# Normalise four feature tiles first, run the second expert pass by tokens, and finish three layer norms late

## The chip, the cores and the metric

One core of a Trainium2 chip runs the whole program in one launch. The metric is device time in microseconds for one execution. Engines are called as in the profile: PE (TensorE matmuls) with PEld (its weight loads), DVE (VectorE), ACT (ScalarE), POOL (GpSimd) and SP (SyncE, which issues the DMAs).

## The reference, cut to what matters

256 tokens of width 1024 (plus 256 context tokens) pass through two blocks. The parts that the change touches:

```python
# block 1
m_l = silu(c) @ w_ada + b_ada            # six vectors of 1024: shift, scale, gate, twice
u_l = (layer_norm(x) * (1 + sc1) + sh1) @ w_in      # and the same for the context, with c_ctx
...                                       # two gated recurrences, w_out, layer norm
y   = peer(...)                           # 16384 experts; gates X[expert, token]
#   = gelu(U t) * gate, then  y[token, :] = sum over experts of X[expert, token] * V[expert, :]
x   = layer_norm(ALPHA * x + g2 * y)
# block 2: 16 meta tokens are put ahead (272 tokens), then twice
h = ln1(ALPHA_2 * h + 0.5 * swiglu(h, ffn1))
h = ln2(ALPHA_2 * h + mix(h @ w_in) @ w_out)
h = ln3(ALPHA_2 * h + 0.5 * swiglu(h, ffn2))
# swiglu: (silu(h @ w_gate) * (h @ w_up)) @ w_down, inner width 2816
```

## The kernel before, in words

Activations lie transposed: features on the 128 partitions, in 8 tiles of 128, tokens along the free axis. Every large product is computed in three matmuls (`mm3`, lines 326 to 328): both operands are split into a rounded part (fp32r) and the rest, and hi·hi, hi·lo and lo·hi are added up in PSUM.

**Weights** come as one stream, the class `Stream`: 512 KB tiles are loaded by SP into a ring of four buffers (`raw`, line 269), ACT writes the rounded part (`wh`, L292) and DVE, for some tiles POOL, the rest (`wl`, L293), two tiles ahead of use, each into a ring of three. A few tiles at the start of each feed-forward network are split earlier into spare buffers (`eh`, `el`), so that its first four tiles are at hand. Tiles of `w_ada` (`wa2`) come through the same ring and are used by DVE alone (`ada2_step`, L589). Pools and semaphores are the framework's; a planner orders the instructions of each engine at build time by program order and by when it takes their inputs to be ready, except where `issue_after` or `keep_in_program_order` binds them. On the chip each engine then runs in that fixed order.

**Front.** SP loads the first 1 MB tile of `w_ada` (`wa[0]`, of eight), then `xlat` and `xctx` (1 MB each), then three more `wa`, two weight tiles, four `wa`, and more weights (lines 469 to 472). DVE and ACT form sums and squares, PE adds them over the partitions (L527, L532), and `ada1_gen` gives shift and scale of four feature tiles a time (L501, L505, L508, L512); generators 0 and 1 serve tiles 0 to 3, 2 and 3 tiles 4 to 7. Lines 560 to 562 subtract the mean and multiply by `rstd` for all 8 tiles, in pieces of four tiles (128x1024), the product for the context on POOL. `modulate` (L543 to L545) gives `xh` and `xl` tile by tile. PE's first product is `fm_gen` (tiles 0 to 3, 512 tokens wide), then `ada1(2)`, `ada1(3)`, `modulate(3)`.

**Second expert pass.** For each of 128 turns, `w` is a 128x1024 tile of V and `x` the 128x256 gates of its 128 experts (`xsplit`, two turns ahead). `vmm` (L1214 to L1216) takes 128 columns of `w` as the stationary operand and the 256 tokens as the moving one, for 8 feature tiles d: 24 matmuls of 256 columns a turn, into four PSUM banks (`yv[d]` is half a bank). In turns 8 to 39 each fourth turn has an `ada2_step`. The last three turns go feature tile by feature tile; each then goes through L1232 (gate and residual) and `Stats.add`.

**Layer norm.** `Stats.add` (L370 to L387) sums tiles and squares; at the eighth tile PE adds them over the partitions with four fp32 products (L377, L378, L379, L383). `Stats.end` makes `r` (L392 to L395, `rsqrt_to`) and normalises the tiles in turn (L393, L400, L406); `to_input` gives the split input of the next product (L423 or L425 on ACT, L426 on POOL, L427), and the instructions named in `W.behind` hold later weight splits back. PE starts the next product with tile 0:

```python
        def ln_out(tp, st, l, j, tag="lnt", bufs=4):
            for k in st.end(eps1[:, 1:2], [hA[:, k] for k in range(8)]):
                n, g, b = hA[:, k], v2(l, f"ln{j}_g", k), v2(l, f"ln{j}_b", k)
                to_input(tp, k, n, g, b, hi_[:, k], lo_[:, k], tag, bufs)
```

This happens twice before the `mixers` and three times before a feed-forward network in block 2 (after `w_out` of each layer, and between the layers). `ffn` computes gate and up of the first two inner tiles together (`p4`, four weight tiles, 96 matmuls), then one inner tile f at a time, and last eight tiles of the down product. PSUM has 8 banks: four in turn for products (`PM`), four for the rest (`PS`; all four hold the sums of the second expert pass).

Of the kernel before, what the change touches and what calls it, by code (L numbers as in the profile page):

```python
# [171 lines left out]
def build(tc, A, out):  # L172
# [3 lines left out]
    with ExitStack() as ctx:  # L176
# [8 lines left out]
        def PS():  # L185
            return psum.tile([128, 512], F32, tag="aux", name="aux")
# [60 lines left out]
        class Stream:  # L247
# [112 lines left out]
        class Stats:  # L360


            def __init__(self, pl, N):
                self.pl, self.N = pl, N
                self.acc = pl.tile([128, N], F32, name="acc")
                self.acc2 = pl.tile([128, N], F32, name="acc2")
                self.k = 0

            def add(self, s):
                N, last = self.N, self.k == 7  # L370
                if self.k == 0:
                    self.s0 = s
                    S.activation(out=self.acc2, in_=s, func=AF.Square)
                else:
                    if last:
                        self.mean, self.ex2 = PS()[:, 0:N], PS()[:, 0:N]
                        T.matmul(self.mean, onesD, self.acc, start=True, stop=False)  # L377
                        T.matmul(self.ex2, onesD, self.acc2, start=True, stop=False)  # L378
                        T.matmul(self.mean, onesD, s, start=False, stop=True)  # L379
                    q = self.pl.tile([128, N], F32, name="sqk", tag="sqk", bufs=2)  # L380
                    S.activation(out=q, in_=s, func=AF.Square)  # L381
                    if last:
                        T.matmul(self.ex2, onesD, q, start=False, stop=True)  # L383
                    else:
                        V.tensor_tensor(self.acc, self.s0 if self.k == 1 else self.acc, s, OP.add)
                        (G if self.k < 5 else V).tensor_tensor(self.acc2, self.acc2, q, OP.add)  # L386
                self.k += 1  # L387

# [50 lines left out]
        with ExitStack() as fctx:  # L439
# [74 lines left out]
            a0 = ada1_gen(0)  # L514
            next(a0)
            a1 = ada1_gen(1)
# [31 lines left out]
            next(a1)  # L548
            for _ in a0:
                pass  # L550
            next(a1)
# [7 lines left out]
            for e in range(2):  # L559
                for a in range(0, 8, 4):  # L560
                    for src, st, op in ((xs[e], mean, OP.subtract), (xn[e], rstd, OP.mult)):
                        (G if e and st is rstd else V).tensor_tensor(xn[e][:, a:a + 4], src[:, a:a + 4], bc(st[:, None, 256 * e:256 * e + 256], [128, 4, 256]), op)
            W.split_to(0)
            modulate(1)

            lbt = const.tile([128, 3, 8], F32, name="lbt")
            V.tensor_tensor(lbt[:, 0], vc("hlb"), vc("hlb"), OP.subtract)
            S.activation(out=lbt[:, 0], in_=lbt[:, 0], func=AF.Exp)
            V.reciprocal(out=lbt[:, 1], in_=lbt[:, 0])
            V.tensor_tensor(lbt[:, 0], lbt[:, 0], lbt[:, 1], OP.mult)  # L570
            V.tensor_tensor(lbt[:, 0], lbt[:, 0], lbt[:, 0], OP.subtract)
            V.tensor_scalar(lbt[:, 0], lbt[:, 0], 0.0, 1.0 - 1e-6, op0=OP.max, op1=OP.min)
            V.tensor_scalar(lbt[:, 1], lbt[:, 0], LB_FLOOR, None, op0=OP.max)
            V.tensor_scalar(lbt[:, 2], lbt[:, 0], -1.0, 1.0, op0=OP.mult, op1=OP.add)
# [81 lines left out]
            for d in range(2):  # L656
# [7 lines left out]
                if d == 0:  # L664

                    gens = [fm_gen(512, ev, 2 * g) for g in range(2)]
                    W.LS = 0
                    next(gens[0])
                    ada1(2)
                    ada1(3)  # L670
                    modulate(3)
                    W.LS = 1
                    next(gens[1])
                    W.LS = 2
# [325 lines left out]
        with ExitStack() as ectx:  # L1000
# [208 lines left out]
            yv = [yacc[d // 2][:, 256 * (d % 2):256 * (d % 2) + 256] for d in range(8)]  # L1209

            def vmm(i2, d, w, x):
                c = slice(128 * d, 128 * d + 128)
                st_, sp_ = i2 == 0 and d % 2 == 0, i2 == 127
                T.matmul(yv[d], w[0][:, c], x[0], start=st_, stop=False, skip_group_check=True)  # L1214
                T.matmul(yv[d], w[0][:, c], x[1], start=False, stop=False, skip_group_check=True)  # L1215
                T.matmul(yv[d], w[1][:, c], x[0], start=False, stop=sp_, skip_group_check=True)  # L1216
            for i2 in range(125):
                w = W.get("s")
                xsplit(i2 + 2)
                x = xs_t.pop(i2)  # L1220
                for d in range(8):
                    vmm(i2, d, w, x)
                if 8 <= i2 < 40 and i2 % 4 == 0:
                    ada2_step(crow2)
# [3 lines left out]
            st = Stats(vp, 256)  # L1228
            for d in (0, 2, 4, 6, 1, 3, 5, 7):
                for i in range(3):  # L1230
                    vmm(125 + i, d, w[i], xs_t[125 + i])
                V.scalar_tensor_tensor(x1[:, d], yv[d], mada[:, 40 + d:41 + d], x1[:, d], op0=OP.mult, op1=OP.add)  # L1232
                st.add(x1[:, d])
# [25 lines left out]
        def ln_out(tp, st, l, j, tag="lnt", bufs=4):  # L1259
            for k in st.end(eps1[:, 1:2], [hA[:, k] for k in range(8)]):  # L1260
                n, g, b = hA[:, k], v2(l, f"ln{j}_g", k), v2(l, f"ln{j}_b", k)
                to_input(tp, k, n, g, b, hi_[:, k], lo_[:, k], tag, bufs)
# [12 lines left out]
        def ffn(l, j, last, after_first):  # L1275
            c0 = 16 if last else 0
            N = 272 - c0
            with tc.tile_pool(name="ffn", bufs=1) as tp:
                ah = tp.tile([128, 22, N], F32R, name="ah")
                al = tp.tile([128, 22, N], F32R, name="al")  # L1280
                for f in range(22):
                    if f == 0:
                        p4 = [PM()[:, 0:N] for _ in range(4)]
                        mm_pair(p4, [W.get("s") for _ in range(4)], c0, late=l == 0 and j == 1)
                        after_first()
# [11 lines left out]
                st = Stats(tp, N)  # L1297
# [10 lines left out]
                if not last:  # L1308
                    ln_out(tp, st, l, j)
# [13 lines left out]
        def mixers(l):  # L1323
            with tc.tile_pool(name="mx", bufs=1) as tp:
# [12 lines left out]
                mix = tp.tile([128, 8, 272], F32, name="mix")  # L1337
# [42 lines left out]
                proj(small_to, conv(0), conv(1), conv(2))  # L1380
                residual(3 * l, hA, hA)
# [76 lines left out]
                def attention(name, m0, qk, scale, v):  # L1458
                    PT = [tp.tile([128, 4, 272 - t0], F32, name=f"{name}T{j}", tag=f"attT{j}") for j, (t0, n) in enumerate(TT)]
                    units = [(0, 0), (1, 0), (1, 2), (2, 0)]  # L1460
                    P, mx = {}, {}
                    for u in units:
# [25 lines left out]
                        P[u] = tp.tile([128, 512], F32, name="attP", tag="attP", bufs=5)  # L1488
# [99 lines left out]
                def z_gate(f):  # L1588
                    def ev(p):
                        zs = tp.tile([128, 272], F32, name="zs", tag="zs", bufs=2)  # L1590
# [41 lines left out]
                st = Stats(tp, 272)  # L1632
# [6 lines left out]
                ln_out(tp, st, l, 2, "xb", 3)  # L1639
# [21 lines left out]
```

## Time and profile before

| | us |
|---|---|
| median of three runs | 2304.39 (2302.50 to 2306.07) |
| the profiled execution | 2302.7, of which the span of the trace is 2300.9 |
| PE busy | 2189.4 (95%) |
| DVE / ACT / POOL busy | 1547.5 / 1148.5 / 534.2 |
| second expert pass, first to last matmul | 832.3 to 1201.4 |

In the rows below a line of the timeline is: start, duration, engine, line, operation, output<-inputs, size, count, and in brackets the idle time ahead of it and what ended that. A matmul's duration is its way through the array; how often one starts is read from the starts of its neighbours. A row of the stretches gives the stretch, its length, the busy time of PE, PEld, DVE, ACT and POOL (with the number of instructions), the clock granted to PE as a share of 2.4 GHz, the share of time that DMA was busy, and GB/s.

### The profile page before, as it was taken

Reading aid. Unit: us, or ns where it says so; the run is one execution under the profiler, and the core shown is the slowest. Engines: PE = TensorE matmul, PEld = TensorE weight load, DVE = VectorE, ACT = ScalarE, POOL = GpSimd, SP = SyncE. Lnnn points to the kernel's source line nnn. Section 1 sums busy time; section 2 is a strip of 40 time slices with the busy share of each in tenths; the row PEclk is TensorE's granted clock in tenths of the full one; section 3 lists DMA queues with packets and bytes.
Section 4 is the critical chain, followed back from the end, with each engine's and each line's share of the span. In section 5 each row is a group of like instructions: output and inputs, shape, how many; then the busy total and the mean of one; then the engine's idle time right before and its main releaser. Section 6 shows DMA issues by size and latency. Waiting matters only on the chain.

```text
span 2300.9 us, 42996 instructions
## 1 busy us (share of the span) xinstructions
PE 2189.4 (95%) x17168; PEld 2116.5 (92%) x17168; DVE 1547.5 (67%) x2722; ACT 1148.5 (50%) x1976; POOL 534.2 (23%) x483
## 2 busy tenths in 40 slices
PE   6898889899999999999999999999999999899998
PEld 4787779899999999999999999889999999889998
DVE  6897869967677766555566556775556555776554
ACT  4455555344444454444445445565445444675443
POOL 2334334558666600000011002110001000302000
PEclk8999999999999999999999999999999999999999
DMA  6642125454444457655564554344564556233554
GB/s 260 230 166 74 56 85 166 138 169 153 148 155 152 152 189 228 201 183 184 182 216 149 174 171 149 101 138 147 174 179 152 174 170 197 92 120 122 188 179 126
DMA packets 102009, 367.55 MB, mean 160 GB/s; under 512 B 11440, under 2 KB 13360, under 8 KB 100528
## 3 DMA queue, kind: packets, MB, share of 16 engines
q1 hardware_dynamic: 101808, 364.80, 49.0%
q8 instruction: 134, 2.20, 0.4%
q14 instruction: 67, 0.55, 0.1%
HBM read 363.71 MB, written 1.05 MB: 159 GB/s over the span
## 4 chain that ended last, share of the span: by engine, by line
PE 83%; DVE 9%; issue 3%; POOL 2%; DMA 1%; ACT 1%; SPq 0%; DVEq 0%; POOLq 0%; ACTq 0%
PE main L328 20%; PE main L327 20%; PE main L326 20%; PE aux L1214 5%; PE aux L1215 5%; PE aux L1216 5%; PE aux L1106 2%; DVE wl L293 1%; DMA raw<-wa 1%; POOL wl L293 1%; DVE raw L589 1%; PE aux L808 1%; DVE acc L386 0%; PE aux L1526 0%; PE aux L1438 0%
## 5 line engine op out<-in xcount | busy, mean ns | idle before, releaser
L292 ACT ACTIVATE wh<-raw 128x1024 fp32r<-128x1024 f32 (+1 forms) x630 | 660.0, 1048 | 905.6 <-PE main L327 354.4
L293 DVE TENSOR_TENSOR wl<-raw,wh 128x1024 fp32r<-128x1024 f32 (+1 forms) x574 | 705.7, 1230 | 456.1 <-ACT wh L292 454.8
L326 PE MATMUL main<-hh,wh 128*128 128x256 f32 (+1 forms) x2856 | 826.7, 290 | 20.2 <-DVE hh L423 14.4
L328 PE MATMUL main<-hh,wl 128*128 128x256 f32 (+1 forms) x2856 | 822.3, 288 | 20.9 <-DVE wl L293 17.1
L327 PE MATMUL main<-hl,wh 128*128 128x256 f32 (+1 forms) x2856 | 821.2, 288 | 1.6 <-DVE hl L332 0.6
L328 PEld LDWEIGHTS main<-hh,wl 128*128 128x128 f32 x2856 | 546.4, 191 | 25.2 <-DVE wl L293 19.6
L326 PEld LDWEIGHTS main<-hh,wh 128*128 128x128 f32 x2856 | 545.6, 191 | 25.3 <-DVE hh L423 16.5
L327 PEld LDWEIGHTS main<-hl,wh 128*128 128x128 f32 x2856 | 545.6, 191 | 3.9 <-DVE hl L427 1.6
L1215 PE MATMUL aux<-xsl,wh 128*128 128x256 f32 x1024 | 290.2, 283 | 0.0
L1216 PE MATMUL aux<-xsh,wl 128*128 128x256 f32 x1024 | 290.0, 283 | 0.0
L1214 PE MATMUL aux<-xsh,wh 128*128 128x256 f32 x1024 | 289.9, 284 | 0.0
L386 POOL TENSOR_TENSOR acc<-acc,sqk 128x272 f32<-128x272 f32 (+1 forms) x32 | 40.7, 1271 | 852.0 <-ACT sqk L381 851.8
L1100 POOL TENSOR_SCALAR oh<-cst,slotT 128x128 f32<-128x128 f32 x256 | 209.8, 835 | 91.6 <-PE aux L1106 83.0
L326 PE MATMUL main<-ah,wh 128*128 128x272 f32 (+1 forms) x704 | 201.9, 287 | 0.0
L327 PE MATMUL main<-al,wh 128*128 128x272 f32 (+1 forms) x704 | 201.8, 287 | 0.0
L328 PE MATMUL main<-ah,wl 128*128 128x272 f32 (+1 forms) x704 | 201.3, 286 | 0.0
L293 POOL TENSOR_TENSOR wl<-raw,wh 128x1024 fp32r<-128x1024 f32 x56 | 151.2, 2704 | 214.5 <-ACT wh L292 203.5
L1215 PEld LDWEIGHTS aux<-xsl,wh 128*128 128x128 f32 x1024 | 196.8, 192 | 0.0
L1216 PEld LDWEIGHTS aux<-xsh,wl 128*128 128x128 f32 x1024 | 196.8, 192 | 0.0
L1214 PEld LDWEIGHTS aux<-xsh,wh 128*128 128x128 f32 x1024 | 196.6, 192 | 0.1
L328 PEld LDWEIGHTS main<-ah,wl 128*128 128x128 f32 x704 | 132.7, 189 | 0.0
L326 PEld LDWEIGHTS main<-ah,wh 128*128 128x128 f32 x704 | 132.6, 188 | 0.0
(470 smaller groups left out, 3138.3 us busy)
## 6 DMA issues: line engine op xcount, KB each, us to landing
raw<-uT SPq DMA_DIRECT2D x128, 512.0 KB, 3.3
raw<-pv SPq DMA_DIRECT2D x128, 512.0 KB, 3.5
raw<-ffn_gate SPq DMA_DIRECT2D x88, 512.0 KB, 3.3
raw<-ffn_up SPq DMA_DIRECT2D x88, 512.0 KB, 3.3
raw<-win SPq DMA_DIRECT2D x72, 512.0 KB, 3.4
raw<-ffn_down SPq DMA_DIRECT2D x64, 512.0 KB, 3.6
raw<-wa SPq DMA_DIRECT2D x32, 512.0 KB, 4.3
raw<-wout SPq DMA_DIRECT2D x24, 512.0 KB, 3.3
```

Source lines behind the costliest of these rows:

```text
L292: S.activation(out=hi[:, :n], in_=t[:, :n], func=AF.Copy)
L293: (G if mode == "p" else V).tensor_tensor(lo[:, :n], t[:, :n], hi[:, :n].bitcast(F32), OP.subtract)
L326: T.matmul(o, lh, rh, start=start, stop=False)
L327: T.matmul(o, lh, rl, start=False, stop=False)
L328: T.matmul(o, ll, rh, start=False, stop=stop)
L386: (G if self.k < 5 else V).tensor_tensor(self.acc2, self.acc2, q, OP.add)
L589: V.scalar_tensor_tensor(w, w, 1.0, c, op0=OP.mult, op1=OP.mult, accum_out=mada[:, 16 + j:17 + j])
L1100: G.tensor_scalar(oh1[:, j], iota, slotT[0][:, t0 + j:t0 + j + 1], None, op0=OP.is_equal)
L1106: T.matmul(pg[:, 128 * j:128 * j + 128], oh1[:, j], oh2[:, j], start=True, stop=True)
L1214: T.matmul(yv[d], w[0][:, c], x[0], start=st_, stop=False, skip_group_check=True)
L1215: T.matmul(yv[d], w[0][:, c], x[1], start=False, stop=False, skip_group_check=True)
L1216: T.matmul(yv[d], w[1][:, c], x[0], start=False, stop=sp_, skip_group_check=True)
```

## The change

Front: `xlat` and `xctx` are loaded ahead of `wa[0]`, and `ada1_gen(0)` and `(1)` run behind the statistics in program order. `normalise(a)` does four feature tiles: tiles 0 to 3 ahead of the first product, all on DVE; tiles 4 to 7 behind the first half of the first group, with the context's product on POOL. The lower bounds `lbt` are computed behind that.

Second expert pass: the gates of 128 tokens are the stationary operand and 512 columns of V the moving one; a turn has 12 matmuls, and `yacc` holds tokens by features. At the end the sums are copied out, transposed back on PE (`features`) and go on as before; `Stats` takes tiles 4 to 7 straight to PE (`pe=4`).

Late normalisation (`behind_norm`): for the norms after both `w_out` and after the second feed-forward network of layer 0, the un-normalised tile times the norm's gain (`gh`, `gl`: `raw_input`) is multiplied by the first four weight tiles, with two more columns (minus gain, and bias). The result is put right afterwards by mean and `r` (`finish`). `Stats` does its four products behind the 12th matmul of the first weight tile. `mix` and the attention's `attP` move into the memory of `gh` and `gl`. From the diff (cut):

```diff
-            load_wa()
             nc.sync.dma_start(xlat, A["xT"])
             nc.sync.dma_start(xctx, A["ctxT"])
-            for _ in range(3):
+            for _ in range(4):
                 load_wa()
...
-            a0 = ada1_gen(0)
-            next(a0)
-            a1 = ada1_gen(1)
+            a0, a1 = ada1_gen(0), ada1_gen(1)
...
+            def normalise(a):
+                for e in range(2):
                     for src, st, op in ((xs[e], mean, OP.subtract), (xn[e], rstd, OP.mult)):
-                        (G if e and st is rstd else V).tensor_tensor(...)
+                        E = G if a and e and st is rstd else V
+                        E.tensor_tensor(xn[e][:, a:a + 4], src[:, a:a + 4], ..., op)
+            normalise(0)
             W.split_to(0)
             modulate(1)
...
                     next(gens[0])
+                    W.split_to(1)
+                    normalise(4)
                     ada1(2)
                     ada1(3)
                     modulate(3)
...
+            def vmm(i2, e, w, x, ts=(0, 1)):
+                f = slice(512 * e, 512 * e + 512)
+                for t in ts:
+                    c = slice(128 * t, 128 * t + 128)
+                    y = yacc[2 * e + t]
+                    T.matmul(y, x[0][:, c], w[0][:, f], start=(i2 == 0), stop=False)
+                    T.matmul(y, x[0][:, c], w[1][:, f], start=False, stop=False)
+                    T.matmul(y, x[1][:, c], w[0][:, f], start=False, stop=(i2 == 127))
...
+            def half(e, t):
+                for i in range(3):
+                    vmm(125 + i, e, w[i], xs_t[125 + i], (t,))
+                if t == 0:
+                    S.activation(out=yt[:, 2 * e], in_=yacc[2 * e], func=AF.Copy)
+                else:
+                    V.tensor_copy(yt[:, 2 * e + 1], yacc[2 * e + 1])
+            def features(e):
+                for d in range(4 * e, 4 * e + 4):
+                    p = PM()[:, 0:256]
+                    for t in range(2):
+                        T.transpose(p[:, 128 * t:128 * t + 128], yt[:, 2 * e + t, c], ident)
+                    V.scalar_tensor_tensor(x1[:, d], p, mada[:, 40 + d:41 + d], x1[:, d], ...)
+                    st.add(x1[:, d])
+            half(0, 0); half(0, 1); half(1, 0); features(0); half(1, 1); features(1)
...
+        def raw_input(l, j, d):
+            S.activation(out=gh[:, d, r], in_=h_, func=AF.Identity, scale=g)
+            V.scalar_tensor_tensor(gl[:, d, r], h_, g, gh[:, d, r], op0=OP.mult, op1=OP.subtract)
+        def behind_norm():
+            def product(i):
+                p = PM()[:, 0:274]
+                hi, lo = W.get("s")
+                for k in range(8):
+                    mm3(p, hi[:, c], lo[:, c], gh[:, k], gl[:, k], k == 0, k == 7)
+                    if (i, k) == (0, 3):
+                        st.reduce()
+            def finish(i):
+                S.activation(out=cb, in_=p[:, 272:274], func=AF.Copy)
+                V.scalar_tensor_tensor(u, ms, cb[:, 0:1], p[:, 0:272], op0=OP.mult, op1=OP.add)
+                V.tensor_tensor(u, u, st.acc2, OP.mult)
+                S.activation(out=u, in_=u, func=AF.Identity, bias=cb[:, 1:2])
+            product(0); product(1)
+            for k in st.end(eps1[:, 1:2], [hA[:, k] for k in range(8)]):
+                to_input(b2, k, ...)       # k == 1: ms = copy of the mean
+                ...                        # k == 2: finish(0); k == 4: finish(1)
+            product(2); product(3); finish(2); finish(3)
```

## Rows read from the trace of the kernel before

**Rows 1.** The page: busy time by engine, and the chain's shares.

```profile
PE 2189.4 (95%) x17168; PEld 2116.5 (92%) x17168; DVE 1547.5 (67%) x2722; ACT 1148.5 (50%) x1976; POOL 534.2 (23%) x483
...
PE 83%; DVE 9%; issue 3%; POOL 2%; DMA 1%; ACT 1%; SPq 0%; DVEq 0%; POOLq 0%; ACTq 0%
```

**Rows 2.** Stretches: length; PE, PEld, DVE, ACT, POOL busy (count); clock; DMA; GB/s.

```profile
37.17:350.00 312.83, 274.66 (x1830) 241.05 (x1831) 258.87 (x406) 164.97 (x267) 117.45 (x70) 0.94 0.35 117
...
832.30:1201.40 369.10, 369.10 (x3075) 368.80 (x3073) 213.02 (x285) 179.68 (x266) 5.53 (x7) 1.00 0.62 198
...
1545.97:1556.71 10.74, 7.13 (x34) 5.92 (x33) 8.69 (x22) 6.04 (x12) 4.04 (x6) 0.84 0.16 50
1556.71:1752.82 196.11, 196.11 (x1561) 196.11 (x1561) 106.14 (x134) 92.31 (x129) 8.50 (x9) 1.00 0.55 175
1752.82:1761.50 8.68, 5.64 (x26) 4.66 (x25) 6.56 (x17) 4.96 (x10) 4.49 (x5) 0.80 0.20 62
...
2093.83:2102.90 9.07, 5.79 (x25) 4.55 (x24) 7.10 (x18) 4.73 (x10) 3.38 (x5) 0.81 0.18 59
```

**Rows 3.** Timeline of PE in the second expert pass, first and last of 49.

```profile
1000.05 0.28 PE L1216 MATMUL aux<-xsh,wl 128*128 128x256 f32 x1
...
1005.81 0.28 PE L1216 MATMUL aux<-xsh,wl 128*128 128x256 f32 x1
```

**Rows 4.** Timeline of PE, matmuls of 512 columns, first and last of 13.

```profile
61.25 0.40 PE L327 MATMUL main<-xl,wh 128*128 128x512 f32 x1
...
63.98 0.39 PE L327 MATMUL main<-xl,wh 128*128 128x512 f32 x1
```

**Rows 5.** Waits, 840 to 1190 us: who waited for whom, us, times, longest.

```profile
ACT wh L292 <- PE aux L1215: 182.1, 121, 1.5
```

**Rows 6.** The page: DMA issues of V, KB each, us from issue to landing.

```profile
raw<-pv SPq DMA_DIRECT2D x128, 512.0 KB, 3.5
```

**Rows 7.** Timeline at the end of the second expert pass, all engines.

```profile
1201.16 0.28 PE L1216 MATMUL aux<-xsh,wl 128*128 128x256 f32 x1
...
1202.21 2.35 POOL L293 TENSOR_TENSOR wl<-raw,wh 128x1024 fp32r<-128x1024 f32 x1 [1.33 <-ACT wh L292]
...
1202.54 2.30 DVE L386 TENSOR_TENSOR acc<-acc,sqk 128x256 f32<-128x256 f32 x1
...
1205.70 1.06 PE L383 MATMUL aux<-sqk,onesD 128*128 128x256 f32 x2
...
1209.57 0.60 PE L326 MATMUL main<-hh,e 128*128 128x272 f32 x1 [2.80 <-DVE hh L423]
```

**Rows 8.** Groups by line and form, 1440 to 1545 us: PE transposes.

```profile
L1411 PE MATMUL aux<-cst,cv 128*128 128x128 f32 x8 | 1.0, 273 | 0.0
```

**Rows 9.** Timeline of the front, all engines.

```profile
7.15 1.93 PE L501 MATMUL aux<-x,cs 128*32 128x512 f32 x8 [3.76 <-DMA x<-wa]
...
9.55 1.23 DVE L524 TENSOR_TENSOR s<-xlat 128x1024 f32<-128x1024 f32 x1 [2.71 <-DMA xlat<-xT]
...
16.89 1.22 DVE L562 TENSOR_TENSOR xn<-xlat,aux 128x1024 f32<-128x1024 f32 x1 [0.40 <-ACT m2a L555]
...
21.36 1.11 PE L532 MATMUL aux<-sq,onesD 128*128 128x256 f32 x4
...
27.41 6.15 POOL L562 TENSOR_TENSOR xctx<-xctx,rstd 128x1024 f32<-128x1024 f32 x2 [26.97 <-ACT rstd L336]
27.98 6.66 DVE L562 TENSOR_TENSOR xn<-xn,rstd 128x1024 f32<-128x1024 f32 x2
...
34.57 0.70 DVE L544 TENSOR_SCALAR xm<-xn,mada 128x256 f32<-128x256 f32 x1
...
37.17 0.79 PE L327 MATMUL main<-xl,wh 128*128 128x512 f32 x1 [3.92 <-DVE xl L545]
```

**Rows 10.** Groups by line and form around the first late norm, 1545.5 to 1562 us.

```profile
L427 DVE TENSOR_TENSOR hl<-t,hh 128x272 fp32r<-128x272 f32 x8 | 3.7, 477 | 1.5 <-POOL t L426 1.1
...
L383 PE MATMUL aux<-sqk,onesD 128*128 128x272 f32 x2 | 0.6, 393 | 0.0
```

More of the change, by code (lines that the diff above doesn't have):

```diff
@@ L360, in build, with __init__ @@
         class Stats:
[L363 to L366, printed above, removed]
+            def __init__(self, pl, N, bufs=1, late=False, pe=7):
+                self.pl, self.N, self.late, self.pe = pl, N, late, pe
+                self.acc = pl.tile([128, N], F32, name="acc", tag="acc", bufs=bufs)
+                self.acc2 = pl.tile([128, N], F32, name="acc2", tag="acc2", bufs=bufs)
                 self.k = 0
@@ L673, in build @@
                     next(gens[1])
+                    lower_bounds()
                     W.LS = 2
@@ L1220, in build @@
                 x = xs_t.pop(i2)
-                for d in range(8):
-                    vmm(i2, d, w, x)
+                for e in range(2):
+                    vmm(i2, e, w, x)
                 if 8 <= i2 < 40 and i2 % 4 == 0:
@@ L1257, in build, with raw_columns @@
         V.memset(onesG, 1.0 / 256)
-        def ln_out(tp, st, l, j, tag="lnt", bufs=4):
+        pending, raw = [], [None, None]
+        def raw_columns(l, j):
+            gh, gl = raw[:] = [b2.tile([128, 8, 274], F32R, name=n, tag=n) for n in ("gh", "gl")]
+            for c, n, s_ in ((272, "g", -1.0), (273, "b", 1.0)):
+                v = v2(l, f"ln{j}_{n}", 0, 8)
+                S.activation(out=gh[:, :, c], in_=v, func=AF.Copy, scale=s_)
+                V.scalar_tensor_tensor(gl[:, :, c], v, s_, gh[:, :, c].bitcast(F32), op0=OP.mult, op1=OP.subtract)
@@ L1264, in mm_pair @@
+                if k == 4:
+                    finish(1)
+            product(2)
+            product(3)
+            finish(2)
+            finish(3)
+            return out_
         def mm_pair(outs, ws, c0, order=range(8), x=(hi_, lo_), late=False):
@@ L1282, in ffn @@
                     if f == 0:
-                        p4 = [PM()[:, 0:N] for _ in range(4)]
-                        mm_pair(p4, [W.get("s") for _ in range(4)], c0, late=l == 0 and j == 1)
+                        if pending:
+                            p4 = [u[:, c0:] for u in behind_norm()]
+                        else:
+                            p4 = [PM()[:, 0:N] for _ in range(4)]
+                            mm_pair(p4, [W.get("s") for _ in range(4)], c0, late=True)
                         after_first()
@@ L1296, in ffn @@
                 ln_exp_table()
-                st = Stats(tp, N)
+                late = not last and j == 3
+                st = Stats(b2, N, 1, late)
+                if late:
+                    raw_columns(l, j)
                 for d in range(8):
@@ L1307, in ffn @@
                     st.add(h_)
-                if not last:
-                    ln_out(tp, st, l, j)
+                    if late:
+                        raw_input(l, j, d)
+                if late:
+                    pending.append((st, l, j))
+                elif not last:
+                    for k in st.end(eps1[:, 1:2], [hA[:, k] for k in range(8)]):
+                        to_input(b2, k, hA[:, k], v2(l, f"ln{j}_g", k), v2(l, f"ln{j}_b", k), hi_[:, k], lo_[:, k], "lnt", 3)
                 else:
```

106 lines of the change are left out of this document (67 added, 39 removed).

## The prediction

> **What bounds the kernel now.** I read the page's shares of busy time and the chain first, then the stretches of the span, then the timeline where PE stands still. PE is busy 95% of the span and carries 83% of the chain [rows 1], so there are two ways to win time: fill the 111.5 us in which PE idles (2300.9 less 2189.4), or make its matmuls fewer. In the second expert pass PE never idles: 369.1 us busy of 369.1 at full clock [rows 2]. There only the matmuls' own pace counts. The other places this change touches are gaps: PE's first real matmul comes at 37.17 us [rows 9], and three layer norms in block 2 leave stretches of 10.74, 8.68 and 9.07 us in which PE is busy 7.13, 5.64 and 5.79 us, at a granted clock of 0.84, 0.80 and 0.81, that is, partly at the lower of its two levels, 1.2 GHz, after it stood still [rows 2].
>
> **Second expert pass: 19.5 us less for the matmuls.** Matmuls of 256 columns start each 5.76 us / 48 = 0.120 us [rows 3]. Matmuls of 512 columns with the same kinds of operand (fp32r, 128x128 stationary, another stationary tile each time) start each 2.73 / 12 = 0.2275 us at full clock [rows 4], not 0.240: some 12 ns a matmul don't grow with its columns. A turn goes from 24 x 0.120 = 2.88 to 12 x 0.2275 = 2.73 us; 1536 x 0.2275 = 349.4 us against 3072 x 0.120 = 368.6, which is 19.2 less. Against the measured 369.1 it is 19.7; rounding of the starts leaves both open by about 1 us either way, and I take 19.5.
>
> The Trainium skill (TensorE: Matmul & The Clock Gate, section Back-to-back issue gap) states that the gap between matmuls of N columns is N/2.4 ns plus about 2.5 ns at full clock. By it 3072 gaps of 109 ns become 1536 of 216 ns, an estimate of 3.8 us gained instead of 19.5. The trace disagrees with the page for this stream: 120 ns, not 109, at 256 columns [rows 3], and 227.5, not 216, at 512 [rows 4]; I go by the rows.
>
> Can the operands keep up with a turn of 2.73 us? DVE is busy 213.0 / 128 = 1.66 us a turn and ACT 1.40 [rows 2], and neither gets more of it. ACT's split waited for PE to free its buffer in 121 of the 128 turns [rows 5]. A tile of V lands 3.5 us after its issue [rows 6] and four buffers give it four turns, 10.9 us, for that and two splits. So supply stays hidden; in the eight turns with an `ada2_step` five tiles must come in 10.9 us, which is 2.2 us each, and there the reserve is least.
>
> **The end of that pass: 2.5 us more.** The sums now lie tokens by features. Behind the last matmul come a copy out of PSUM (128x512, at most twice a 272-wide DVE operation of 0.477 us [rows 10]: 0.95), and before it on DVE up to 1 us left over from `features(0)`, whose nine operations of about 0.45 us don't fit beside the six 512-column matmuls and transposes that cover them. Then transposes (16 x 0.125 us = 2.0 us on PE [rows 8], half of them ahead of the last group of matmuls), and four tiles that each need two fp32 products, at 0.5 us each (0.6 for one by itself [rows 10]): 4.0 us, where before the four products of the end were all that was left. Before, the last square's product starts at 1205.70, 4.5 us behind the last matmul at 1201.16 [rows 7]. Of this, about 1.9 us went into a DVE addition that took 2.30 us beside a POOL subtraction of 2.35 [rows 7]; with `pe=4` no such addition stands there. After: 1.0 + 0.95 + 0.5 (first transposes and gate) + 4.0 + 0.6 = 7.0 us, and 1 us of transposes ahead of the last group: 3.5 more, or, where DVE clears in time, 1.5. I take 2.5. The norm behind it is unchanged. Net for the pass: 17.
>
> **Front: 7 us less.** `xlat` landed at 9.55 us, one megabyte behind `wa[0]` at 7.15 [rows 9]; loaded first it lands some 2.4 us earlier and `xctx` too. `wa[0]` moves back two places in SP's queue, by 2 x 2.4 us, but `wa[1]` to `wa[3]`, on which generators 0 and 1 end, come behind the same bytes as before. So the statistics gain 2.4 us, and perhaps 1 us more, since their last matmuls (21.36 [rows 9]) no longer run among generator work. From `rstd`, ready at 27.41, to the first `xl` DVE and POOL do both halves of the context and the latent: 6.66 us for two DVE products that take 1.22 us each when POOL is quiet (the row at 16.89 is the same shape), because POOL's two (6.15 us) run beside them [rows 9]. Now DVE does two of 1.22 us for tiles 0 to 3 and goes on to `modulate`; PE then starts 2.6 us after the first `xm` (34.57 to 37.17), as before. That is 6.66 - 2.44 = 4.2 us less. One POOL product of about 3 us is left for tiles 4 to 7, and as the planner may put it first, DVE can lose up to 3 us to it; a weight subtraction (1.2 us) can also fall between. Together 2.4 + 1 + 4.2 = 7.6 at the most likely order, 2.4 if POOL and the shifts eat the rest, 11 if the weight split slips behind too. I take 7. Tiles 4 to 7 then fall where DVE had little to do, behind the first 24 matmuls; `lbt` is small work that only has to be there by the first gates. From 37 to 350 us DVE is busy 258.9 of 312.8 us and PE 274.7 [rows 2]: neither is full, the stages hang on one another, so an earlier start moves them all.
>
> The Trainium skill (SBUF — State Buffer, section SBUF: two separate sides) has the lock that this looks like: a DVE operation with two SBUF inputs and a GpSimd operation that reads SBUF don't share, the second blocks until the first ends. By it the one POOL product that stays can cost its whole length, about 3 us, and the front would give 4 rather than 7; the trace agrees with the lock at 1202.54, 2.30 us for a 256-wide addition [rows 7].
>
> **Three late norms: 9 us less.** What a gap costs now: its length, less its main matmuls at 196.11 / 1561 = 0.1256 us [rows 2], less the four statistic products that remain (2.0 us at 0.5). The first stretch holds 34 PE instructions, of which 8 are the statistics (each product is two) and 2 straddle its edges: 10.74 - 24 x 0.1256 - 2.0 = 5.7. The second: 8.68 - 16 x 0.1256 - 2.0 = 4.7. The third: 9.07 - 15 x 0.12 - 2.0 = 5.3. Sum 15.7: the ceiling, for PE that never waits. Added: two columns in 272 are nothing, but the last network has 256 columns and now gets 274 in four weight tiles: 96 x 0.0056 = 0.5 us. `raw_input` adds an ACT and a DVE operation (about 0.6 and 0.48 us) per tile; beside 24 matmuls, 3.0 us, DVE comes to about 3.0 us a tile behind `w_out`, so up to 0.5 us may be late; behind the down product (66 matmuls, 8.3 us) it is hidden. For the last tile the wait for `gl` is covered: 21 matmuls and the statistics (2.6 + 2.0 us) stand ahead of its use.
>
> What is late next: PE has 96 x 0.126 + 2.0 = 14.1 us of work behind the last tile, and its next matmuls need the eighth normalised tile 2.6 us later, at 16.7. DVE starts the norm at about 3.6 us, spends some 2.3 us to the first normalised tile, then 10 us on eight tiles (three operations of 0.45 us each, 10.8, of which one or two lie ahead) and 4 x 0.47 = 1.9 us on `finish(0)` and `(1)`, so the eighth is there at 17.8. Behind it the held-back weight subtraction (1.2 us) reaches 19.0, and the second product of that inner tile wants it at 18.3. So 1.1 + 0.7 = 1.8 us wait, each time, 5.4 in all; PSUM banks come free earlier, at `finish(0)`. 15.7 - 0.5 - 5.4 - 0.8 (DVE behind `w_out`) = 9. Bounds: 15 if the planner finds room, 2 if `finish` and the splits queue badly.
>
> **Sum.** 17 + 7 + 9 = 33 us off the profiled execution's 2302.7 us: 2269.7. The median of the runs is 1.7 above it, so 2271 us.
>
> **Rivals.**
> - *The pass gains nothing*, because what a matmul costs beyond its columns doubles with them (0.240 us each): 2302.7 + 2.5 - 16 + 1.7 = 2291. For it: no 512-column stream of V as the moving operand is in the trace. Against: in [rows 4] all kinds of operand are alike, at full clock. (The Trainium skill's gap rule above is a milder form of it, with an estimate of 2287.)
> - *The norms give nothing*: DVE is late by the whole 5 us each time, 2280. For it: DVE has 8.69 us of work in 10.74 already [rows 2] and gets more. Against: PE gets 12 us of work that needs none of it.
> - *The front is taken back later*: an earlier start meets loads that are not there; 2278. For it: neither PE nor DVE is full from 37 to 350 us, so one slow transfer there can take up a head start. Against: DMA is busy 0.35 of that stretch [rows 2], and its ring places are freed by work that starts earlier as well.
> - *Slower: the ring of four is late in every turn of the second pass.* Place: SP's issue of V's next tile, which waits for DVE's subtraction. Each 0.1 us by which a turn exceeds 2.73 costs 12.8 us; from 2.99 us a turn all 33 us are gone, and at 3.1 the time is 2271 + 47 = 2318. Against: the same ring fed turns of 2.88 us with ACT always waiting for PE [rows 5], at 198 GB/s [rows 2], and 2.73 needs 209.
> - *It doesn't do what it says*: pass and norms both give nothing and the front's 7 us pay for the pass's longer end: 2304.4 - 7 + 2.5 = 2300.
>
> **How the numbers follow.** The forecast 0.62 (own range 2261 to 2281); norms give nothing 0.12; front taken back 0.12; pass gains nothing 0.06; nothing in sum 0.04; slower 0.04. A difference under 0.2%, 4.6 us, can't be told from none in this kernel. Faster by more: 0.92; within: 0.04; slower: 0.04. The range takes in the bounds of front and norms and the first three rivals: 2256 to 2288.
>
> **What would show it.** Starts of 512-column matmuls in the pass 0.2275 us apart (0.24: the first rival), the pass 350 us long, ACT still waiting for PE; from its last matmul to the next product some 10 to 11 us instead of 8.4; PE's first `xl` matmul near 30 us; no idle PE and clock 1.0 behind each `w_out`, and a wait for `hl` of about 1 us some 14 us later. It is wrong if PE waits for `wl` in the pass, or if the time stays above 2288.

## The result, and the profile after

The changed kernel takes 2282.8 us (median of four executions, 2274.6 to 2283.0) against 2304.7: ratio 0.9891, 95% interval 0.988 to 0.9903: 21.9 us less by the medians, 25 by the ratio. The forecast was 2271 us, 33.4 less, with a range of 2256 to 2288. Two more measurements of the same kernel (below, again and again_2) gave 0.9879 [0.9862, 0.9897] and 0.9876 [0.986, 0.9893]; over the 12 executions its mean is 2280.0 us and they spread from 2274.6 to 2283.5. So the gain is about 27 us, some 6 less than forecast, and the first three unprofiled executions lay at the high end.

The profiled execution took 2274.6 us (span 2272.5). The page's shares after, to be read beside [rows 1]:

```profile
PE 2171.7 (96%) x15660; PEld 2037.1 (90%) x15660; DVE 1576.2 (69%) x2776; ACT 1167.2 (51%) x2035; POOL 527.8 (23%) x479
...
PE 80%; DVE 11%; issue 4%; ACT 2%; POOL 2%; DMA 1%; SPq 0%; POOLq 0%; DVEq 0%; ACTq 0%
```

The stretches that answer to [rows 2]: the second expert pass, then each late norm from the last matmul of the product before it to the point where PE no longer waits:

```profile
829.49:1178.97 349.48, 349.48 (x1547) 289.00 (x1546) 220.09 (x279) 180.26 (x264) 0.79 (x1) 1.00 0.64 205
1527.96:1548.30 20.34, 19.21 (x140) 18.15 (x139) 19.27 (x45) 16.87 (x36) 6.43 (x9) 1.00 0.17 56
1731.22:1751.50 20.28, 19.15 (x140) 18.09 (x139) 17.72 (x42) 16.69 (x36) 7.23 (x9) 1.00 0.17 56
2068.40:2088.70 20.30, 18.98 (x140) 17.96 (x139) 19.29 (x45) 16.83 (x36) 6.42 (x9) 1.00 0.18 58
```

PE is busy all through the pass, 349.5 us instead of 369.1, and ACT still waits for it, as in [rows 5]. In this trace the clock in the norms is 1.00 where it was 0.80 to 0.84 (the last section has others), and PE idles 1.1 to 1.3 us in 20 where it idled 3.0 to 3.6 in 9 to 11.

PE in the pass, first and last of 16 matmuls of 512 columns, and who waited from 840 to 1170 us (us, times, longest):

```profile
999.62 0.39 PE L1232 MATMUL aux<-wh,xsh 128*128 128x512 f32 x1
...
1003.02 0.39 PE L1232 MATMUL aux<-wh,xsh 128*128 128x512 f32 x1
```

```profile
ACT xsh L331 <- PE aux L1233: 163.9, 122, 1.4
```

(1003.02 - 999.62) / 15 = 0.2267 us from start to start.

Where the 28.4 us between the spans of the two profiled executions come from, read as the shift of the same instruction in both traces:

| stretch | us |
|---|---|
| up to the pass's first matmul (832.33, now 829.49) | -2.8 |
| the pass, first to last matmul (368.83, now 349.25) | -19.6 |
| its end, last matmul to next product (8.41, now 12.44) | +4.0 |
| the three late norms | -3.7, -2.7, -2.6 |
| all the rest behind the pass | -1.0 |

### The profile page after: what moved, and what is told of

It is laid out like the page before. It is cut to its first block, busy times and chain, and to the rows that moved or that the text cites. A ratio compares the mean times of both kernels' runs of the same rounds, so it can differ in the third digit from the quotient of the medians.

```text
span 2272.5 us, 40212 instructions
## 1 busy us (share of the span) xinstructions
PE 2171.7 (96%) x15660; PEld 2037.1 (90%) x15660; DVE 1576.2 (69%) x2776; ACT 1167.2 (51%) x2035; POOL 527.8 (23%) x479
## 4 chain that ended last, share of the span: by engine, by line
PE 80%; DVE 11%; issue 4%; ACT 2%; POOL 2%; DMA 1%; SPq 0%; POOLq 0%; DVEq 0%; ACTq 0%
PE main L328 19%; PE main L326 19%; PE main L327 19%; PE aux L1233 5%; PE aux L1232 5%; PE aux L1234 5%; PE aux L1122 3%; DVE wl L293 2%; DVE raw L602 1%; POOL wl L293 1%; PE aux L824 1%; ACT wh L292 0%; PE aux L1632 0%; PE aux L1543 0%; DMA raw<-win 0%
## 5 line engine op out<-in xcount | busy, mean ns | idle before, releaser
L328 PE MATMUL main<-hh,wl 128*128 128x256 f32 (+1 forms) x2808 | 807.9, 288 | 22.2 <-DVE wl L293 18.3
L326 PE MATMUL main<-hh,wh 128*128 128x256 f32 (+1 forms) x2808 | 812.5, 290 | 12.4 <-DVE hh L436 5.7
L327 PE MATMUL main<-hl,wh 128*128 128x256 f32 (+1 forms) x2808 | 805.8, 287 | 1.9 <-DVE hl L440 0.8
L327 PEld LDWEIGHTS main<-hl,wh 128*128 128x128 f32 x2808 | 534.8, 190 | 4.1 <-DVE hl L440 1.8
L388 POOL TENSOR_TENSOR acc<-acc,sqk 128x272 f32<-128x272 f32 (+1 forms) x29 | 37.3, 1287 | 1210.8 <-ACT sqk L381 1210.7
L1232 PE MATMUL aux<-wh,xsh 128*128 128x512 f32 x512 | 199.3, 390 | 0.0
L1233 PE MATMUL aux<-wl,xsh 128*128 128x512 f32 x512 | 199.3, 389 | 0.0
L1234 PE MATMUL aux<-wh,xsl 128*128 128x512 f32 x512 | 199.2, 389 | 0.0
L331 ACT ACTIVATE xsh<-X 128x256 fp32r<-128x256 f32 x128 | 53.4, 418 | 166.1 <-PE aux L1233 164.3
L327 PEld LDWEIGHTS main<-al,wh 128*128 128x128 f32 x704 | 132.2, 188 | 0.0
L1119 DVE TENSOR_SCALAR oh<-cst,slotT,slotT 128x128 f32<-128x128 f32 x256 | 80.6, 357 | 55.3 <-PE aux L1122 55.3
```

Source lines behind the costliest of these rows:

```text
L326: T.matmul(o, lh, rh, start=start, stop=False)
L327: T.matmul(o, lh, rl, start=False, stop=False)
L328: T.matmul(o, ll, rh, start=False, stop=stop)
L331: S.activation(out=hi, in_=src, func=AF.Copy)
L1119: V.tensor_scalar(oh2[:, j], iota, slotT[1][:, t0 + j:t0 + j + 1], slotT[2][:, t0 + j:t0 + j + 1], op0=OP.is_equal, op1=OP.mult)
L1232: T.matmul(y, x[0][:, c], w[0][:, f], start=(i2 == 0), stop=False)
```

## The experiments

All kernels of one group ran on one chip beside the kernel before, whose executions there spread from 2302.4 to 2311.1 us. Ratios are to it, and "us less" is worked out from the ratio.

**The parts by themselves, and the whole once more.**

> The changed kernel once more, nothing edited. Its profiled execution took 2274.6 us, the other three 2282.7 to 2283.0. Theory A: an execution falls into one of two courses some 8 us apart; the repeat shows times near 2274.6 and near 2282.8 and nothing between, most of them the longer one, and if its profile falls into the longer course, one stage of the trace carries the whole 8 us as idle PE. Rival B: the first time was a stray; all times lie from 2281 to 2285. Rival C: the times are spread evenly from 2274 to 2284, many small delays.

Measured: 2278.9 us (2277.4 to 2282.5), 0.9879 [0.9862, 0.9897]. There are no two groups: with the first four and again_2, twelve executions in all fill 2274.6 to 2283.5 without a gap of 2 us. C holds.

Front alone: the diff's hunks ahead of the second expert pass.

> The kernel before with the front's part of the change alone (the loading order, four tiles normalised ahead of the others, the lower bounds later). Forecast on record: 7 us less. My theory now: in the trace of the changed kernel PE's first product with xl comes 5.1 us earlier, but behind 320 us only 2.8 us of it are left, so alone it gives 2.8 us: 2301.9 as a median. Rival: the loss is a matter of the two other parts (they do not touch the front, but the planner's times do), and alone it gives 5 us or more: 2299 or less. Second rival: the longer course of the changed kernel comes from the front; then this median is 5 us above the kernel before, near 2310, while its shortest time is 2.8 below.

Measured: 2303.0 against 2306.9, 0.9983 [0.9974, 0.9992]; 3.9 us less, 1.8 to 6.0 by the interval. That holds the theory's 2.8 and the first rival's 5, and not the 7 on record. The eleven executions, 2301.2 to 2305.8, show no longer course.

Pass alone: `vmm`, `half`, `features` and `Stats`.

> The kernel before with the second expert pass by tokens alone, and its statistics with four tiles taken to PE. Forecast on record: 17 us less (matmuls 19.5 less, the end 2.5 more). My theory now: 15.6 less (matmuls 19.6 less, the end 3.9 more, because POOL's weight subtraction blocks a DVE addition there): 2289.1. Rival: the pass at 209 GB/s is where the longer course of the changed kernel comes from, a tile of V that is late now and then; then the median is some 2297 and the trace or the times show two groups 8 us apart.

Measured: 2290.3 (2285.6 to 2296.0, without two groups), 0.9926 [0.991, 0.9943], 17 us less; the interval holds both the 17 on record and the 15.6. The matmuls take 349.24 us in this trace, the end 13.78.

Norms alone: `behind_norm`, `raw_input`, `raw_columns` and the buffers, and with them the order of the first products behind the norms that stay as they were.

> The kernel before with the three late norms alone (and the order of the first products behind the norms that stay as they were). Forecast on record: 9 us less. My theory now: 9.1 less for the three norms and 0.5 to 1.5 for the order of the products behind the other norms: 2294 to 2295. Rival: some of it needs the other parts (other PSUM banks and buffers at that time), and alone it gives 5 or less: 2300.

Measured: 2296.7, 0.9962 [0.9948, 0.9976], 8.8 us less (10.2 by the medians), 5.5 to 12.0 by the interval: the 9 on record, not the rival's 5 or less. The three parts add up to 29.8, the whole gives 27.9: within their intervals they are additive, and only the front lies clearly below its forecast.

**Three suspected costs taken away.** The changed kernel did not run in this group; its ratios in the others are 0.9876 to 0.9891.

```diff
-                        E = G if a and e and st is rstd else V
+                        E = V
```

> The changed kernel with the context product of tiles 4 to 7 on DVE instead of POOL. In the trace of the changed kernel POOL runs it at 23.60 us for 3.38 us, and DVE's product beside it takes 3.36 us instead of 1.23; shift and scale of tiles 0 to 3 (mada, L524) wait behind it until 27.98. So the first product with xl comes 2 to 3 us earlier here, near 29.5 us. Theory A: what reaches the end is the advance of the second half's scale (the last mada, 49.36 us now), which hangs on PE's order: 39 main matmuls and 64 halves of the generators' products stand ahead of it; PE starts earlier but waits for DVE's shifts, so the last mada moves by 1 us or less and so does the time: 0 to -1 us against the changed kernel. Rival B: a head start of PE's first product stays as it is: -2.5 us.

Measured: 2279.8, 0.9874 [0.9858, 0.9891]. The first product with `xl` comes at 29.99 us, 2.0 earlier, the last `mada` at 48.44 (0.9 to 2.5 earlier than in the six other traces with that front); the pass begins at 832.75, not earlier. The `mada` moved more than A allows. The times can't tell A from B: the interval reaches 3.8 us to either side.

```diff
+                    W.split_to(W.ahead(W.i + 1))
+                    W.dma_to(W.ahead(W.i + 3))
-                    next(gens[1])
+                    with tc.issue_after(adal[0].ins):     # adal: last product of the generators
+                        next(gens[1])
```

> The changed kernel with the second tile's first 24 matmuls held behind the last product of the generators 2 and 3 on PE, so that 24 main matmuls stand ahead of the last mada and not 39: it comes near 45 us instead of 49.36, and the first product with xl stays at 32. Theory A (the front's gain is the advance of the last mada, since DVE is busy nearly all the time behind it until 160 us): -3.5 to -4.5 us against the changed kernel. Rival B (DMA issues nothing from 40 to 53 us and the ring's loads come in too late behind it, so an earlier mada meets weights that are not split): within 1 us of the changed kernel. Rival C (holding matmuls back costs PE more than it gives): +1 to +3 us.

Measured: 2280.8, 0.9887 [0.987, 0.9903]; no gain is seen. The last `mada` came at 48.20, not 45: the two generators run one behind the other on PE, and PE waits 0.8 us for each `row`. The pass begins at 831.87. So A's condition wasn't met, and with an interval of 3.9 us to either side none of the three is refuted; that late loads are the cause, as B has it, isn't shown.

```diff
-                    specs.append((A[n + "_up"][l, i], "p" if i == 0 else "s"))
+                    specs.append((A[n + "_up"][l, i], "p" if i == 0 and (l or n == "ffn2") else "s"))
```

> The changed kernel with the subtraction of the first up tile of the first feed-forward network on DVE instead of POOL. In the trace of the changed kernel POOL runs it at 1179.00 us for 2.61 us, DVE's addition of squares beside it takes 2.56 us instead of about 0.42, and the copy of the sums out of PSUM waits behind that. Theory A (that lock made the end of the second pass 3.9 us longer than before and not 2.5): the end, from the pass's last matmul to the next product, goes from 12.3 to about 10.2 us, -2 us in all. Rival B: DVE's own 1.2 us subtraction takes the place, so -1 or less. Rival C: the end hangs on PE's transposes and the statistics' products in their order, and nothing changes.

Measured: 2277.9, 0.9865 [0.9849, 0.9882]; the end of the pass 11.46 us instead of 12.44. Rival B: the addition is short again (0.42 us), but the last copy of the sums now waits behind DVE's own subtraction of 1.23 us and three additions, 2.4 us behind the last matmul:

```profile
1180.79 0.40 PE L1234 MATMUL aux<-wh,xsl 128*128 128x512 f32 x1
...
1181.00 1.23 DVE L293 TENSOR_TENSOR wl<-raw,wh 128x1024 fp32r<-128x1024 f32 x1
...
1183.15 0.69 DVE L1255 COPY X<-aux 128x512 f32<-128x512 f32 x1
```

> The changed kernel with all three edits: the context product of tiles 4 to 7 on DVE, the second tile's first matmuls behind the generators, the first up tile's subtraction on DVE. If the theories A hold: first product with xl near 29.5 us, last mada near 43 to 45 us, 10.2 us from the second pass's last matmul to the next product; together -6 to -7 us against the changed kernel, some 2274 us. If the loads of the ring bound the stage behind the front, only the end's 2 us are left.

Measured: 2277.6, 0.9872 [0.9855, 0.9888]. Last `mada` at 46.53, pass begun at 830.25, its end 11.85 us. That isn't the 2274 of the theories A. The `mada` was 3.7 us earlier than on the mean of the six traces with the changed front, the pass 1.4; but the pass of those six begins at 829.3 to 834.7.

**The front taken out, the end mended.**

> The changed kernel with the front as it was before: pass by tokens and late norms alone. Theory A (the front is worth 3.5 us, as the first matmul of the second pass comes 3.5 us earlier on the mean of four traces with the changed front than of three with the old one): 3 to 4 us above the changed kernel, and its pass begins between 832 and 839 us. Rival B (nothing of the front is left behind 330 us): equal to the changed kernel. Rival C (the forecast on record): 7 us above it.

Measured: 2282.3 against 2279.7 for the changed kernel beside it, 0.9902 [0.9885, 0.9919] against 0.9876 [0.986, 0.9893]: 2.6 us by the medians, 6 by the ratios. A fits best; the intervals overlap, so neither B nor C is excluded by this pair alone. Its pass begins at 834.85.

To the hunk of end_dve come two more:

```diff
-                if t == 0:
+                if t == 0 or e == 1:
                     S.activation(out=yt[:, 2 * e + t], in_=yacc[2 * e + t], func=AF.Copy)
...
+        with tc.issue_after(W.behind[0].ins):
             S.activation(out=sel, in_=selr.rearrange("p (h c) -> p h c", h=8), func=AF.Copy)
```

> The changed kernel with the first up tile's subtraction on DVE, the last copy of the pass's sums on ACT instead of DVE, and the rounding of sel on ACT held behind the norm's second tile. With the subtraction alone, the last copy waited on DVE from 1181.0 to 1183.15 us behind a weight subtraction and three additions, and the rounding of sel (1.06 us) stood ahead of the logarithm of the variance. Theory A (DVE's queue sets the end of the pass): the copy starts within 0.3 us of the last matmul, and the end goes from 11.5 to about 9 us; with that, 3.4 us less than the changed kernel. Rival B (PE's eight late statistics products and the wait between them set it): 11 us still.

Measured: 2278.2, 0.9879 [0.9862, 0.9895]; the end of the pass 9.64 us, 2.8 less. A holds for the place, if not to the full 3.4 us; in the times 2.8 us can't be told from their spread.

> The kernel end_act with the context product of tiles 4 to 7 on DVE as well. Expected: the end of the pass as in end_act (9 us), the first product with xl near 30 us and the last mada near 48.4 us; 1 us less than end_act at most. About 2275 to 2276 us where the changed kernel has 2279.

Measured: 2274.3 (2273.3 to 2276.5), 0.9859 [0.9843, 0.9876], the lowest of all kernels here and 5.5 us below the changed kernel beside it; the intervals of the two overlap. End of the pass 9.64, first `xl` product 29.96, last `mada` 48.36, pass begun at 829.73.

> The changed kernel, nothing edited, beside the other three on one chip. Executions of one kernel have spread over 8 us so far; the traces put that between 50 and 340 us and into the few places where PE stands still and comes back at the lower clock. Expected: times from 2275 to 2283, the pass's own length 349.24 us and its end 12.44 us as in the two traces there are, and the difference from them in the time at which the pass begins and in the norms' and mixers' gaps behind it.

Measured: 2279.7 (2275.7 to 2283.5), 0.9876. Pass 349.24 us, begun at 834.66; its end was 13.77 us, not 12.44, and the rows of it below say why.

## Why the prediction was right, and where it was not

**The pass's matmuls: right.** 19.5 us forecast, 19.6 in every trace with the new pass (349.22 to 349.25 us). The Trainium skill (TensorE: Matmul & The Clock Gate, section Back-to-back issue gap) gives N/2.4 ns plus about 2.5 for a matmul by itself, by which an estimate of 4 us would be gained; for a stream of weight loads and matmuls it has about 131 ns at 512 columns, which the prediction left out. The trace agrees with neither: 227 ns at 512 columns and 120 at 256 [rows 3], so about 13 ns a matmul don't grow with the columns here.

**The late norms: right.** 9 us forecast, 9.0 in the profiled pair (3.7, 2.7, 2.6); in six of the eleven traces with these norms it is 1.5 or 3 us less, for a reason of the clock that the forecast did not have (last section). The wait forecast for the eighth normalised tile and the weight subtraction behind it was 1.8 us a norm, some 16.7 us behind the last tile. PE there, the first norm; the last matmul of `w_out` was at 1527.96:

```profile
1542.00 0.29 PE L328 MATMUL main<-gh,e 128*128 128x274 f32 x1
...
1544.65 0.29 PE L328 MATMUL main<-hh,wl 128*128 128x272 f32 x1
1545.16 0.39 PE L326 MATMUL main<-hh,wh 128*128 128x272 f32 x1 [0.23 <-ACT hh L438]
1545.71 0.39 PE L327 MATMUL main<-hl,wh 128*128 128x272 f32 x1 [0.16 <-DVE hl L440]
...
1546.34 0.29 PE L327 MATMUL main<-hl,wh 128*128 128x272 f32 x1
1547.37 0.40 PE L328 MATMUL main<-hh,wl 128*128 128x272 f32 x1 [0.74 <-DVE wl L293]
```

From 1544.65 to 1547.37 stand six steps that take 6 x 0.126 = 0.76 us elsewhere and 2.72 here: 2.0 us lost, 16.7 us behind the last tile, on `hh` and `hl` first and then on `wl`.

**The end of the pass: right in kind, too small.** +2.5 forecast with bounds 1.5 and 3.5; it is +4.0, and +5.4 in three of seven traces of that code. The step that failed is "with `pe=4` no such addition stands there". The additions of the second to fourth squares still do, and one on DVE meets POOL's subtraction; all engines, changed kernel:

```profile
1178.74 0.40 PE L1234 MATMUL aux<-wh,xsl 128*128 128x512 f32 x1
...
1179.00 2.61 POOL L293 TENSOR_TENSOR wl<-raw,wh 128x1024 fp32r<-128x1024 f32 x1 [0.34 <-ACT wh L292]
...
1179.32 2.56 DVE L388 TENSOR_TENSOR acc<-acc,sqk 128x256 f32<-128x256 f32 x1
1181.81 0.68 DVE L1255 COPY X<-aux 128x512 f32<-128x512 f32 x1
1182.41 0.41 DVE L388 TENSOR_TENSOR acc<-acc,sqk 128x256 f32<-128x256 f32 x1
...
1182.54 0.55 PE L1262 MATMUL main<-cst,X 128*128 128x128 f32 x3 [2.27 <-DVE X L1255]
```

An addition of this size takes 0.41 us when POOL is quiet and 2.56 beside it; the last copy starts 3.1 us behind the last matmul, where 1 us was allowed, and PE stands still 2.27 us. In end_dve, where the subtraction stands on DVE instead, the copy still came 2.4 us behind, and 1.23 of them are the subtraction: without either some 1 us is left, as allowed. The same place in end_act, where neither POOL nor DVE is in the way of the copy:

```profile
1178.53 0.40 PE L1234 MATMUL aux<-wh,xsl 128*128 128x512 f32 x1
...
1179.22 0.58 ACT L1253 ACTIVATE X<-aux 128x512 f32<-128x512 f32 x1
1179.85 0.66 PE L1262 MATMUL main<-cst,X 128*128 128x128 f32 x4 [0.48 <-ACT X L1253]
```

Its end is 9.64 us, 1.2 more than before. The transposes and late products cost more than that, since the end before held a DVE addition of 2.30 us beside POOL [rows 7]; how much by themselves wasn't measured.

**The front: half of it.** 7 us forecast, bounds 2.4 to 11. The first product with `xl` came 5.1 us earlier in the profiled pair, not 7.6 as in the likeliest order. `rstd` came 3.9 us earlier (23.55 instead of 27.41), where 3.4 were allowed; 2.1 us went to DVE's product beside POOL's, and 1.2 to a weight subtraction, both of which the prediction had named as possible:

```profile
23.55 1.23 DVE L572 TENSOR_TENSOR xn<-xn,rstd 128x1024 f32<-128x1024 f32 x1 [1.45 <-ACT rstd L336]
23.60 3.38 POOL L572 TENSOR_TENSOR xctx<-xctx,rstd 128x1024 f32<-128x1024 f32 x1 [23.16 <-ACT rstd L336]
24.70 3.36 DVE L572 TENSOR_TENSOR xctx<-xctx,rstd 128x1024 f32<-128x1024 f32 x1
27.98 0.15 DVE L524 SCALAR_TENSOR_TENSOR mada<-aux,vec 128x4 f32<-128x4 f32 x1
...
28.12 1.21 DVE L293 TENSOR_TENSOR wl<-raw,wh 128x1024 fp32r<-128x1024 f32 x1
```

The planner put POOL's product for tiles 4 to 7 ahead of DVE's. The Trainium skill (SBUF — State Buffer, section SBUF: two separate sides) has this lock, and the trace agrees: 3.36 us here, 1.23 for DVE's first row, and 2.0 us came back at the first `xl` product when POOL's went to DVE. But only a part of the head start reached the end, and that is the step that failed: "neither is full, the stages hang on one another, so an earlier start moves them all". Fourteen traces, by their front:

| front | traces | first `xl` product | last `mada` | pass begins |
|---|---|---|---|---|
| before | before, pass_alone, norms_alone, no_front | 36.7 to 37.3 | 51.4 to 52.4 | 832.3, 838.7, 834.0, 834.9 |
| changed | after, again, again_2, front_alone, end_dve, end_act | 31.9 to 32.2 | 49.4 to 50.9 | 829.5, 832.5, 834.7, 832.4, 831.5, 829.3 |
| product on DVE | lock_dve, best | 30.0 | 48.4 | 832.8, 829.7 |
| generators first | ada_bound, three_edits | 31.8, 30.1 | 48.2, 46.5 | 831.9, 830.3 |

On the mean of the six traces against the four, 5.0 us at the first product are 1.8 at the last `mada`, 2.5 at the first statistics product of the norm ahead of the expert passes (318.3 less 315.8 us) and 3.3 at the pass (835.0 less 831.6); front_alone measured 3.9. Traces of one front begin the pass up to 6 us apart, so no more can be read than that 2 to 4 us are left. The loss lies ahead of the last `mada`, and a part of it can be named: scale and shift of tiles 4 to 7 hang on the generators' products, and on PE these stand between main matmuls in an order fixed when the program is built, 39 ahead of the last one instead of 32, and 7 more at 0.2275 us are 1.6 of the 3.2 us lost; with 24 ahead, in ada_bound, it came another 2.0 us earlier. Behind the last `mada` DVE is full in many slices, though not in all; stretches of the changed kernel, in the columns of [rows 2]:

```profile
60.00:70.00 10.00, 8.69 (x39) 6.80 (x38) 9.80 (x14) 6.02 (x10) 3.59 (x3) 1.00 0.61 203
70.00:80.00 10.00, 9.70 (x43) 7.71 (x42) 10.00 (x10) 2.29 (x3) 4.12 (x2) 1.00 0.65 217
80.00:90.00 10.00, 10.00 (x45) 8.26 (x44) 8.64 (x19) 3.12 (x6) 0.00 (x0) 1.00 0.80 256
90.00:100.00 10.00, 10.00 (x84) 9.96 (x83) 7.09 (x10) 9.97 (x11) 2.40 (x1) 1.00 0.82 286
100.00:110.00 10.00, 5.96 (x35) 5.56 (x35) 9.29 (x10) 4.70 (x7) 1.02 (x1) 0.83 0.60 197
110.00:120.00 10.00, 10.00 (x85) 10.00 (x85) 10.00 (x10) 5.34 (x7) 2.18 (x1) 1.00 0.53 171
120.00:130.00 10.00, 9.98 (x85) 9.78 (x84) 10.00 (x17) 5.28 (x10) 0.00 (x0) 1.00 0.50 159
130.00:140.00 10.00, 6.47 (x43) 6.06 (x43) 10.00 (x16) 3.67 (x7) 0.00 (x0) 0.87 0.83 304
```

The average of 258.9 in 312.8 us, on which the prediction rested, hid these full slices. That they take anything back isn't shown: the mean lead is no smaller behind them, and the stretch from the last `mada` to the pass varies from 779.9 to 786.7 us among these traces, more than what was to be seen in it. Nor is it shown that the 2.0 us of lock_dve are lost: at that statistics product lock_dve and best stand at 313.6 and 314.1 us, 1.9 earlier on the mean than the six (313.7 to 317.3), and lock_dve then loses some 3 us at half clock (last section). So the rival "front taken back later" held for about half of the front, but the part that can be named stands in PE's order, and a late load, as the rival has it, isn't shown.

**Rivals.** Pass without gain, norms without gain, ring of four late, nothing in sum: all false. The time lies above the forecast's own range by 1.8 us in the first measurement and inside it (2278.9, 2279.7) in the two others.

## What to carry to other kernels

Halving the count of matmuls at the same columns pays what does not grow with the columns, and can be read beforehand from the starts of neighbours in a stream of the same operands. A head start of the first product is worth only what it moves of the inputs that come next: look at what stands ahead of them in each engine's order, and don't take a stage's mean busy share as a sign that all of it moves. A tail of small operations behind a long product should have no long two-input operation of DVE or POOL in it, and its copies belong on the engine with the empty queue; the end went from 12.44 to 9.64 us so.

## What the runs showed that was not expected

Executions of one kernel differ by up to 9 us, and the clock is part of it. The end of the pass in again_2, where every instruction stands as in the changed kernel's rows above; PE, and the stretch behind its wait in again_2 and then in the changed kernel's first trace:

```profile
1187.70 0.90 PE L1262 MATMUL main<-cst,X 128*128 128x128 f32 x3 [2.28 <-DVE X L1255]
1188.40 1.06 PE L395 MATMUL aux<-acc,onesD 128*128 128x256 f32 x2
...
1190.96 0.62 PE L379 MATMUL aux<-x,onesD 128*128 128x256 f32 x2
```

```profile
1187.70:1190.96 3.26, 3.26 (x10) 2.72 (x10) 1.55 (x4) 0.81 (x2) 0.00 (x0) 0.50 0.51 163
```

```profile
1182.54:1185.36 2.82, 2.82 (x14) 2.15 (x15) 1.55 (x4) 1.23 (x3) 0.00 (x0) 1.00 0.59 189
```

PE had stood still 2.28 us in the one and 2.27 in the other; in the first the granted clock behind it was 0.50 (1.2 GHz) for 3.3 us, in the second 1.00 (2.4 GHz). The end took 13.77 us against 12.44. It is 13.75 to 13.78 in three of the seven traces with this code and 12.43 to 12.45 in four. The same at 318 us, lock_dve and then again, with no difference in what the kernels do there:

```profile
318.00:325.00 7.00, 5.50 (x13) 4.43 (x14) 4.87 (x15) 3.60 (x8) 2.56 (x4) 0.55 0.23 75
```

```profile
318.00:325.00 7.00, 3.86 (x17) 2.83 (x18) 5.58 (x17) 4.60 (x11) 3.68 (x3) 1.00 0.45 150
```

Lock_dve is 3.2 us ahead there, so the two stretches don't hold the same work; but from the first matmul behind the wait of PE (3.15 us in lock_dve, 3.14 in again) to the next main product it needs 13.6 us (319.50 to 333.05) and again 10.6 (322.67 to 333.30). So lock_dve lost what it had been ahead, some 3 us.

The late norms show it too. The second one in again, just behind the waits for `hh`, `hl` and `wl`, and the same place in the changed kernel's first trace:

```profile
1754.70:1758.10 3.40, 3.40 (x18) 3.40 (x17) 2.92 (x5) 2.77 (x5) 0.00 (x0) 0.51 0.52 154
```

```profile
1751.01:1754.41 3.40, 3.40 (x30) 3.40 (x29) 2.92 (x5) 3.40 (x6) 0.00 (x0) 1.00 0.53 154
```

From the last product ahead of a late norm to the first down product behind it, the three norms together take 404.6 to 404.7 us in five of the eleven traces that have them, 406.1 to 406.4 in five with one such stretch, 407.7 in end_dve with two, and 413.7 to 414.0 in the three traces without late norms. So the wait that the prediction allowed 1.8 us for can cost 1.5 us more, and the norms give some 9.2, 7.6 or 6.2 us by execution.

So a short wait of PE costs its length and, in some executions and not in others, a stretch at half clock behind it: a price that a single profile shows or hides, and a reason to compare traces place by place and times over many executions.
